# Row sums on one core: a tail of 10 rows in place of 16, whose last piece is shared by two adders

## The chip, the core and the metric

The kernel runs on one core of a Trainium2 chip. The metric is the device time of one execution in microseconds (us), as the median of several runs. The engines that appear here are VectorE (DVE), ScalarE (ACT), GpSimd (POOL) and SyncE (SP). SP issues every DMA of this kernel, so all of them stand in one queue, which 16 DMA engines work off.

## The reference

```python
def setup_inputs():
    batch, seq, dim = 32, 512, 1024
    return {"x": np.random.randn(batch, seq, dim).astype(np.float32), "divisor": float(dim)}

def reference(x, divisor):
    return (np.sum(x, axis=-1) / divisor).astype(np.float32)
```

The input has 16,384 rows of 1,024 numbers, 67.1 MB in all; each row is summed and scaled by 1/1024.

## The kernel before, in words

Each of the 128 partitions gets 128 rows of `D` = 1024 numbers. `F` = 15 of them come from the front of `x` (`x_first`, results in `res0`); the other `W` = 113 lie behind one another for each partition, and of these `M` = 97 form the main part (`x_main`, results in `res`) and the last `L` = 16 the tail (`x_last`, results in `fin`; `res` and `fin` are parts of one tile, `every`).

The list `loads` holds the large loads in order: the main part in loads of 2, five times 16, and 15 rows, then the 15 rows of `x_first`, then the first two loads of the tail. They rotate over three buffers `bulk0` to `bulk2` of 16 rows. The first two are issued at the very start. SP issues each later one when the adders are done with the buffer's previous load (the third waits for the first to land instead). Then SP issues two small loads of the tail, `pa` (into the tile `tail`) and `pb`, which have places of their own. Loads follow one another in the queue in this order.

Two adders share the rows. DVE sums all rows of a large load with one reduction (`reduce_sum`, line 217), but in the last main load and in `x_first` ACT takes the last 4 and 6 rows, one activation with an accumulated output for each (`row_on_act`, line 185). DVE's reductions write unscaled sums, which POOL scales (lines 159 and 163). In the tail DVE takes single rows with `both_halves` (line 207): one operation adds the first half of a row to its second half and accumulates over the columns, in two instructions, the main one and an accumulator read. ACT takes other rows of the tail.

The tail's pieces do not end at row ends; their limits are in `ends` and set by `c10`, `c14` and `c15`. Row 10 is split over the two tail loads: DVE sums its head into `part` and adds that when it sums the rest. Of row 14, ACT sums the head into a column just ahead of `pa`, and then sums that column and the rest as one piece. DVE sums row 15's head, at the end of `pa`, into a column just behind `pb`, and then sums `pb` with that column and a zero that POOL wrote at the start. A carry of this kind increments the semaphore of the piece that it is added to, so that the adder waits for 16 increments of the load and one of the carry: ACT's on `in_pa`, DVE's on `in_pb`.

Three stores take the results out: `o_first` (line 149) after POOL's scaling, `o_main` (line 152) with all columns of `every` up to `E` as soon as all but the last two rows are done, and `o_last` (line 240) with the remaining columns when both adders have counted up `done`.

Of the kernel before, what the change touches and what calls it, by code (L numbers as in the profile page):

```python
# [10 lines left out]
AX = mybir.AxisListType.X  # L11
# [24 lines left out]
def kernel(  # L36
# [6 lines left out]
    nc = tc.nc  # L43
    nc.at_finalize(start_loads_at_once)
    xf = x.flatten_outer_dims()
    N, D = xf.shape
    P = nc.NUM_PARTITIONS
    scale = 1.0 / float(divisor)
    J = N // P
    assert J * P == N  # L50

    F, L = 15, 16
    M = J - F - L
    W = M + L
    x_first = bass.AP(tensor=x.tensor, offset=0, ap=[[F * D, P], [1, F * D]])
    x_main = bass.AP(tensor=x.tensor, offset=P * F * D, ap=[[W * D, P], [1, M * D]])
    x_last = bass.AP(tensor=x.tensor, offset=P * F * D + M * D, ap=[[W * D, P], [1, L * D]])
    o_first = bass.AP(tensor=out.tensor, offset=0, ap=[[F, P], [1, F]])
    E = M + L - 2
    o_main = bass.AP(tensor=out.tensor, offset=P * F, ap=[[W, P], [1, E]])  # L60
    o_last = bass.AP(tensor=out.tensor, offset=P * F + E, ap=[[W, P], [1, 2]])

    def room(name, *shape):
        return nc.alloc_sbuf_tensor(name, [P, *shape], F32).ap()
# [5 lines left out]
    bulk = [room(f"bulk{i}", 16 * D) for i in range(3)]  # L70
# [1 line left out]

    c10, c14, c15 = 640, 288, 608
    ends = [0, 10 * D + c10, 14 * D + c14, 15 * D + c15, 16 * D]
    tail = room("tail", 7 * 256)
    pa, row14 = tail[:, 256 : 256 + ends[3] - ends[2]], tail[:, 255 : 256 + D - c14]
    pb = room("pb", 512)[:, : D - c15 + 2]
    part = room("part", 1)  # L80
    res0 = room("res0", F)
    every = room("every", W)
    res, fin = every[:, :M], every[:, M:]
# [4 lines left out]
    loads = []  # L88
    sems = {}

    def sem(name):
        sems[name] = nc.alloc_semaphore(name)
        return sems[name]

    in_bulk = [sem(f"in_bulk{i}") for i in range(3)]
    in_pa, in_pb = (sem(f"in_{n}") for n in ("pa", "pb"))
    out_first, out_main = sem("out_first"), sem("out_main")
    dve, act, pool = sem("by_dve"), sem("by_act"), sem("by_pool")
    done = sem("done")
    landed = nc.alloc_semaphore("landed")  # L100

    main = [(2, 0)] + [(16, 0)] * 5 + [(15, 4)]
    first = [(15, 6)]
    assert sum(r for r, _ in first) == F and sum(r for r, _ in main) == M
    for rows_of, src, dst in ((main, x_main, res), (first, x_first, res0)):
        j = 0
        for rows, on_act in rows_of:
            t = bulk[len(loads) % 3][:, : rows * D]
            loads.append((t, in_bulk[len(loads) % 3], src[:, j * D : (j + rows) * D], on_act, dst[:, j : j + rows]))
            j += rows  # L110
    for k in range(2):
        t = bulk[len(loads) % 3][:, : ends[k + 1] - ends[k]]
        loads.append((t, in_bulk[len(loads) % 3], x_last[:, ends[k] : ends[k + 1]], 0, None))


    for t, s, src, *_ in loads[:2]:
# [6 lines left out]
    done_dve, done_act = {}, {}  # L123
    a = 0
    for k, (t, s, src, on_act, dst) in enumerate(loads[:-2]):
        a += on_act
        done_dve[k], done_act[k] = k + 1, a
    arrived, seen = [], {}
    for t, s, *_ in loads:
        seen[s.num] = seen.get(s.num, 0) + 16  # L130
# [4 lines left out]
    for k, (t, s, src, *_) in enumerate(loads):  # L135
# [7 lines left out]
                nc.sync.wait_ge(act, done_act[k - 3])  # L143
            nc.sync.wait_ge(s, arrived[k] - 16)
        nc.sync.dma_start(out=t, in_=src).then_inc(s, 16)
    nc.sync.dma_start(out=pa, in_=x_last[:, ends[2] : ends[3]]).then_inc(in_pa, 16)
    nc.sync.dma_start(out=pb[:, : D - c15], in_=x_last[:, ends[3] : ends[4]]).then_inc(in_pb, 16)
    nc.sync.wait_ge(pool, 3)
    nc.sync.dma_start(out=o_first, in_=res0).then_inc(out_first, 16)
    nc.sync.wait_ge(act, done_act[len(loads) - 3] + 5)  # L150
    nc.sync.wait_ge(dve, done_dve[len(loads) - 3] + 10)
    nc.sync.dma_start(out=o_main, in_=every[:, :E]).then_inc(out_main, 16)


    nc.gpsimd.memset(pb[:, D - c15 :], 0.0).then_inc(pool)  # L155
    k = len(main) - 1
    nc.gpsimd.wait_ge(dve, done_dve[k])
    nc.gpsimd.wait_ge(act, done_act[k])
# [5 lines left out]


    (t8, s8, *_), (t9, s9, *_) = loads[-2:]
    head10, rest10 = t8[:, 10 * D :], t9[:, : D - c10]
    head14 = t9[:, 4 * D - c10 :]

    def row8(r):  # L170
        return t8[:, r * D : (r + 1) * D]

    def row9(r):
        return t9[:, (r - 10) * D - c10 : (r - 9) * D - c10]

    a = 0

    def row_on_act(src, by, dst, count=act):  # L180
        nonlocal a
        if a >= len(junk):
            nc.scalar.wait_ge(act, a - len(junk) + 1)
        scratch = junk[a % len(junk)][:, : src.shape[-1]]
        nc.scalar.activation(scratch, src, COPY, scale=by, accum_out=dst).then_inc(count)  # L185
        a += 1

    for k, (t, s, src, on_act, dst) in enumerate(loads[:-2]):
        rows = t.shape[1] // D
# [2 lines left out]
                nc.scalar.wait_ge(s, arrived[k])  # L192
            row_on_act(t[:, r * D : (r + 1) * D], 1.0, dst[:, r : r + 1])
    nc.scalar.wait_ge(s8, arrived[-2])
    for r in range(6, 10):
        row_on_act(row8(r), scale, fin[:, r : r + 1])
    nc.scalar.wait_ge(s9, arrived[-1])
    row_on_act(row9(13), scale, fin[:, 13:14])
    row_on_act(head14, 1.0, row14[:, :1], in_pa)
    nc.scalar.wait_ge(in_pa, 17)  # L200
    row_on_act(row14, scale, fin[:, 14:15], done)

    def both_halves(dst, src, by=scale, ahead=0.0):
        h = src.shape[-1] // 2
        return nc.vector.tensor_tensor_reduce(  # L207
            out=src[:, :h], in0=src[:, :h], in1=src[:, h:], scale=by, scalar=ahead,
            op0=ADD, op1=ADD, accum_out=dst,
        )  # L210

    d = 0
    for k, (t, s, src, on_act, dst) in enumerate(loads[:-2]):
        m = t.shape[1] // D - on_act
        nc.vector.wait_ge(s, arrived[k])
        rows = t[:, : m * D].rearrange("p (r d) -> p r d", d=D)
        nc.vector.reduce_sum(out=dst[:, :m], in_=rows, axis=AX).then_inc(dve)  # L217
        d += 1
    nc.vector.wait_ge(s8, arrived[-2])
    both_halves(part, head10).then_inc(dve)  # L220
    d += 1
    ahead10 = d
    for r in range(6):
        both_halves(fin[:, r : r + 1], row8(r)).then_inc(dve)
        d += 1
    nc.vector.wait_ge(s9, arrived[-1])
    nc.vector.wait_ge(dve, ahead10)
    both_halves(fin[:, 10:11], rest10, ahead=part).then_inc(dve)
    for r in (11, 12):
        both_halves(fin[:, r : r + 1], row9(r)).then_inc(dve)  # L230
    d += 3
    nc.vector.wait_ge(in_pa, 17)
    nc.vector.wait_ge(pool, 1)
    both_halves(pb[:, D - c15 : D - c15 + 1], pa[:, D - c14 :], 1.0).then_inc(in_pb)
    nc.vector.wait_ge(in_pb, 17)
    both_halves(fin[:, 15:], pb).then_inc(done)


    nc.sync.wait_ge(done, 2)
    nc.sync.dma_start(out=o_last, in_=every[:, E:]).then_inc(landed, 16)  # L240
    for s in (out_main, out_first):
# [40 lines left out]
```

## Time and profile before

| what | value |
|---|---|
| median of 3 runs | 160.26 us (160.24 to 160.31) |
| the profiled execution, its time | 160.4 us |
| its span, from the first to the last instruction | 159.1 us |
| DVE busy | 116.7 us (73%) |
| ACT busy | 18.6 us (12%) |
| POOL busy | 1.0 us (1%) |
| the loads' and stores' queue | 67.18 MB, 98.2% of 16 engines' span |
| read from HBM | 67.11 MB, 422 GB/s over the span |

The span begins with the first instruction of the program and ends with its last. In the views, a line such as L207 is a line of the kernel file; a helper's operations all have the helper's line, so rows are told apart by their tiles, their shapes and their order. `CUSTOM_DVE_ANT_0` is the main instruction of `both_halves` (its shape shows half the columns that it sums), `DVE_READ_ACCUMULATOR2_ANT` its accumulator read. `SPq` lines are DMA issues, and their duration is that of the issue alone. Buffer numbers are left out of names, so `bulk` is any of the three buffers.

### The profile page before, as it was taken

To read this page: it belongs to the slowest core of one execution; us is meant where nothing else is said; L and a number is where in the kernel's file an instruction comes from. 1 tells how busy PE (TensorE), PEld (TensorE's weight loads), DVE (VectorE), ACT (ScalarE), POOL (GpSimd) and SP (SyncE) were. 2 spreads that over 40 slices of the span, in tenths; PEclk is the share of its full clock that TensorE was granted. 3 is DMA by queue.
4 is the path that set the end of the run, shared out by engine and by line. 5 is a ranking of instruction groups with operands and counts; after the bars stand their busy time and mean duration, and the time that the engine had idled before them with its cause. 6 is when DMAs were issued, how large, how long until landed. Compare 5 with 4: busy or idle time off the path is not lost.

```text
span 159.1 us, 145 instructions
## 1 busy us (share of the span) xinstructions
DVE 116.7 (73%) x32; ACT 18.6 (12%) x35; POOL 1.0 (1%) x7
## 2 busy tenths in 40 slices
DVE  0500009999499994999949999499989990399296
ACT  3000000000000000000000000000009100392196
POOL 0000000000000000000000000000000001000000
DMA  7996996997979969969969969959995999889794
GB/s 249 542 527 264 527 527 264 527 461 330 527 346 445 527 264 527 527 264 527 527 264 527 527 264 527 494 247 494 494 494 247 494 494 494 350 350 525 311 421 169
DMA packets 2161, 67.18 MB, mean 422 GB/s; under 512 B 625, under 2 KB 753, under 8 KB 881
## 3 DMA queue, kind: packets, MB, share of 16 engines
q1 hardware_dynamic: 2160, 67.18, 98.2%
q14 instruction: 1, 0.00, 0.0%
HBM read 67.11 MB, written 0.07 MB: 422 GB/s over the span
## 4 chain that ended last, share of the span: by engine, by line
DMA 67%; DVE 31%; another core or an unknown queue 1%; issue 0%
DMA bulk<-in_x_dram 67%; DVE every L217 29%; DVE bulk L207 1%; DVE pb L207 0%; DVE tail L207 0%; DVE every L207 0%
## 5 line engine op out<-in xcount | busy, mean ns | idle before, releaser
L217 DVE TENSOR_REDUCE every<-bulk 128x16 f32<-128x16384 f32 (+2 forms) x7 | 100.3, 14325 | 31.2 <-DMA bulk<-in_x_dram 31.2
L185 ACT ACTIVATE junk<-bulk 128x1024 f32<-128x1024 f32 (+1 forms) x16 | 15.6, 972 | 136.9 <-DMA bulk<-in_x_dram 136.8
L217 DVE TENSOR_REDUCE res<-bulk 128x9 f32<-128x9216 f32 x1 | 9.8, 9754 | 6.3 <-DMA bulk<-in_x_dram 6.3
L207 DVE CUSTOM_DVE_ANT_0 bulk<-bulk 128x512 f32<-128x512 f32 (+1 forms) x9 | 5.5, 664 | 3.1 <-DMA bulk<-in_x_dram 3.1
L185 ACT ACTIVATION_READ_ACCUMULATOR junk<-bulk 128x1 f32 x16 | 3.0, 186 | 0.0
L185 ACT ACT_TABLE_LOAD x1 | 1.3, 1283 | 1.9 <-PEq L120 1.9
L159 POOL TENSOR_SCALAR every<-every 128x97 f32<-128x97 f32 x1 | 0.5, 465 | 129.5 <-DVE every L217 129.5
L207 DVE DVE_READ_ACCUMULATOR2_ANT every<- 128x1 f32 x10 | 0.8, 82 | 0.0
L185 ACT ACTIVATE junk<-tail 128x737 f32<-128x737 f32 x1 | 0.8, 789 | 0.0
L207 DVE CUSTOM_DVE_ANT_0 bulk<-bulk,part 128x192 f32<-128x192 f32 x1 | 0.4, 420 | 0.2 <-DMA bulk<-in_x_dram 0.2
L207 DVE CUSTOM_DVE_ANT_0 tail<-tail 128x304 f32<-128x304 f32 x1 | 0.5, 476 | 0.0
L207 DVE CUSTOM_DVE_ANT_0 pb<-pb 128x209 f32<-128x209 f32 x1 | 0.4, 379 | 0.1
L163 POOL TENSOR_SCALAR res<-res 128x15 f32<-128x15 f32 x1 | 0.3, 263 | 15.7 <-DVE res L217 15.7
L185 ACT ACTIVATION_READ_ACCUMULATOR junk<-tail 128x1 f32 x1 | 0.2, 185 | 0.0
L155 POOL MEMSET pb<- 128x2 f32 x1 | 0.1, 100 | 1.5 <-POOLq L120 1.5
L263 POOL MEMSET const-bfloat16-1.0<- 128x1 bf16 x1 | 0.1, 102 | 0.0
L263 POOL MEMSET const-uint8-127<- 128x1 uint8 x1 | 0.1, 101 | 0.0
L263 POOL MEMSET const-float32-0.0<- 128x1 f32 x1 | 0.1, 98 | 0.2 <-issue 0.2
L263 POOL MEMSET const-float32-1.0<- 128x1 f32 x1 | 0.1, 98 | 0.0
L207 DVE DVE_READ_ACCUMULATOR2_ANT pb<- 128x1 f32 x1 | 0.1, 83 | 0.0
L207 DVE DVE_READ_ACCUMULATOR2_ANT part<- 128x1 f32 x1 | 0.1, 81 | 0.0
## 6 DMA issues: line engine op xcount, KB each, us to landing
bulk<-in_x_dram SPq DMA_DIRECT2D x2, 7680.0 KB, 38.9
bulk<-in_x_dram SPq DMA_DIRECT2D x1, 5440.0 KB, 31.9
bulk<-in_x_dram SPq DMA_DIRECT2D x1, 1872.0 KB, 23.5
bulk<-in_x_dram SPq DMA_DIRECT2D x1, 1024.0 KB, 4.9
tail<-in_x_dram SPq DMA_DIRECT2D x1, 672.0 KB, 24.8
pb<-in_x_dram SPq DMA_DIRECT2D x1, 208.0 KB, 24.9
bulk<-in_x_dram SPq DMA_DIRECT2D x5, 40.7
out_dram<-every SPq DMA_DIRECT2D x1, 55.5 KB, 1.6
```

The lines of the kernel that those rows point to most:

```text
L155: nc.gpsimd.memset(pb[:, D - c15 :], 0.0).then_inc(pool)
L159: nc.gpsimd.tensor_scalar_mul(out=res, in0=res, scalar1=scale).then_inc(pool)
L163: nc.gpsimd.tensor_scalar_mul(out=res0, in0=res0, scalar1=scale).then_inc(pool)
L185: nc.scalar.activation(scratch, src, COPY, scale=by, accum_out=dst).then_inc(count)
L207: return nc.vector.tensor_tensor_reduce(out=src[:, :h], in0=src[:, :h], in1=src[:, h:], scale=by, scalar=ahead, op0=ADD, op1=ADD, accum_ou ...
L217: nc.vector.reduce_sum(out=dst[:, :m], in_=rows, axis=AX).then_inc(dve)
L263: nc = _bacc.Bacc("TRN2", target_bir_lowering=False, num_devices=1)
```

## The change

The tail has 10 rows instead of 16. Of the six rows that leave it, five go to the first load (7 rows instead of 2) and one to the last main load (16 instead of 15, of which DVE sums 12 and ACT 4). `M` becomes 103.

The tail's columns are no longer loaded in order. Its first load begins inside row 3 (from column 340 of that row) and goes to the end of row 9; its second holds rows 0 and 1 and 144 columns of row 2; then `p3` holds columns 144 to 983 of row 2; and the last piece, `p4`, holds the last 40 columns of row 2 and the first 340 of row 3, so it lies in the middle of the tail's data. ACT finishes row 2 from it and DVE row 3.

Four carried sums belong to that piece. DVE sums the rest of row 3 into a column behind the piece, and two parts of row 2 (`row2_y`, 144 columns, and `row2_u`, 640 columns) into columns ahead of it; ACT sums a third part of row 2 (`row2_v`, 200 columns). All four carries and the load increment one semaphore, `in_p4`, and both last additions wait for 16 + 4. DVE's last addition covers 342 columns (340, a carry and a zero), ACT's 43 (3 carries and 40).

In the load of `x_first`, DVE sums its 9 rows one at a time with `both_halves` instead of with one reduction. The last store takes the 8 columns of rows 2 to 9, and `o_main` the columns up to row 1; it waits for 3 rows of ACT and 5 of DVE behind the large loads.

```diff
-    F, L = 15, 16
+    F, L = 15, 10
...
-    E = M + L - 2
+    E = M + 2
...
-    c10, c14, c15 = 640, 288, 608
-    ends = [0, 10 * D + c10, 14 * D + c14, 15 * D + c15, 16 * D]
-    tail = room("tail", 7 * 256)
-    pa, row14 = tail[:, 256 : 256 + ends[3] - ends[2]], tail[:, 255 : 256 + D - c14]
-    pb = room("pb", 512)[:, : D - c15 + 2]
-    part = room("part", 1)
+    y2, u2, a2, c3 = 144, 640, 40, 340
+    ends = [3 * D + c3, L * D, 0, 2 * D + y2, 3 * D - a2]
+    p3 = room("p3", 1024)[:, : ends[4] - ends[3]]
+    n4 = a2 + c3
+    piece = room("piece", 768)
+    p4 = piece[:, 256 : 256 + n4]
+    row2_end, row3_head = piece[:, 253 : 256 + a2], piece[:, 256 + a2 : 256 + n4 + 2]
...
-    main = [(2, 0)] + [(16, 0)] * 5 + [(15, 4)]
+    main = [(7, 0)] + [(16, 0)] * 5 + [(16, 4)]
...
+        by_rows = k == len(loads) - 3
+        done_dve[k], done_act[k] = k + (t.shape[1] // D - on_act if by_rows else 1), a
...
-    nc.sync.dma_start(out=pa, in_=x_last[:, ends[2] : ends[3]]).then_inc(in_pa, 16)
-    nc.sync.dma_start(out=pb[:, : D - c15], in_=x_last[:, ends[3] : ends[4]]).then_inc(in_pb, 16)
+    nc.sync.dma_start(out=p3, in_=x_last[:, ends[3] : ends[4]]).then_inc(in_p3, 16)
+    nc.sync.dma_start(out=p4, in_=x_last[:, ends[4] : ends[0]]).then_inc(in_p4, 16)
...
-    nc.sync.wait_ge(act, done_act[len(loads) - 3] + 5)
-    nc.sync.wait_ge(dve, done_dve[len(loads) - 3] + 10)
+    nc.sync.wait_ge(act, done_act[len(loads) - 3] + 3)
+    nc.sync.wait_ge(dve, done_dve[len(loads) - 3] + 5)
...
-    nc.gpsimd.memset(pb[:, D - c15 :], 0.0).then_inc(pool)
+    nc.gpsimd.memset(row3_head[:, c3 + 1 :], 0.0).then_inc(pool)
...
+    every_carry = 16 + 4
...
     nc.scalar.wait_ge(s8, arrived[-2])
-    for r in range(6, 10):
+    for r in (8, 9):
         row_on_act(row8(r), scale, fin[:, r : r + 1])
     nc.scalar.wait_ge(s9, arrived[-1])
-    row_on_act(row9(13), scale, fin[:, 13:14])
-    row_on_act(head14, 1.0, row14[:, :1], in_pa)
-    nc.scalar.wait_ge(in_pa, 17)
-    row_on_act(row14, scale, fin[:, 14:15], done)
+    row_on_act(row1, scale, fin[:, 1:2])
+    nc.scalar.wait_ge(in_p3, 16)
+    row_on_act(row2_v, 1.0, row2_end[:, 2:3], in_p4)
+    nc.scalar.wait_ge(in_p4, every_carry)
+    row_on_act(row2_end, scale, fin[:, 2:3], done)
...
+            for r in range(m):
+                both_halves(dst[:, r : r + 1], t[:, r * D : (r + 1) * D], 1.0).then_inc(dve)
     nc.vector.wait_ge(s8, arrived[-2])
-    both_halves(part, head10).then_inc(dve)
...
-    for r in range(6):
+    both_halves(row3_head[:, c3 : c3 + 1], row3_rest, 1.0).then_inc(in_p4)
+    for r in (4, 5, 6, 7):
         both_halves(fin[:, r : r + 1], row8(r)).then_inc(dve)
...
     nc.vector.wait_ge(s9, arrived[-1])
-    nc.vector.wait_ge(dve, ahead10)
-    both_halves(fin[:, 10:11], rest10, ahead=part).then_inc(dve)
-    for r in (11, 12):
-        both_halves(fin[:, r : r + 1], row9(r)).then_inc(dve)
...
-    nc.vector.wait_ge(in_pa, 17)
+    both_halves(row2_end[:, :1], row2_y, 1.0).then_inc(in_p4)
+    both_halves(fin[:, :1], row0).then_inc(dve)
+    nc.vector.wait_ge(in_p3, 16)
     nc.vector.wait_ge(pool, 1)
-    both_halves(pb[:, D - c15 : D - c15 + 1], pa[:, D - c14 :], 1.0).then_inc(in_pb)
-    nc.vector.wait_ge(in_pb, 17)
-    both_halves(fin[:, 15:], pb).then_inc(done)
+    both_halves(row2_end[:, 1:2], row2_u, 1.0).then_inc(in_p4)
+    nc.vector.wait_ge(in_p4, every_carry)
+    both_halves(fin[:, 3:4], row3_head).then_inc(done)
```

More of the change, by code (lines that the diff above doesn't have):

```diff
@@ L58 @@
     o_first = bass.AP(tensor=out.tensor, offset=0, ap=[[F, P], [1, F]])
-    E = M + L - 2
+    E = M + 2
     o_main = bass.AP(tensor=out.tensor, offset=P * F, ap=[[W, P], [1, E]])
-    o_last = bass.AP(tensor=out.tensor, offset=P * F + E, ap=[[W, P], [1, 2]])
+    o_last = bass.AP(tensor=out.tensor, offset=P * F + E, ap=[[W, P], [1, W - E]])
     def room(name, *shape):
@@ L95 @@
     in_bulk = [sem(f"in_bulk{i}") for i in range(3)]
-    in_pa, in_pb = (sem(f"in_{n}") for n in ("pa", "pb"))
+    in_p3, in_p4 = (sem(f"in_{n}") for n in ("p3", "p4"))
     out_first, out_main = sem("out_first"), sem("out_main")
@@ L111 @@
     for k in range(2):
-        t = bulk[len(loads) % 3][:, : ends[k + 1] - ends[k]]
-        loads.append((t, in_bulk[len(loads) % 3], x_last[:, ends[k] : ends[k + 1]], 0, None))
+        t = bulk[len(loads) % 3][:, : ends[2 * k + 1] - ends[2 * k]]
+        loads.append((t, in_bulk[len(loads) % 3], x_last[:, ends[2 * k] : ends[2 * k + 1]], 0, None))
     for t, s, src, *_ in loads[:2]:
@@ L126 @@
         a += on_act
-        done_dve[k], done_act[k] = k + 1, a
+        by_rows = k == len(loads) - 3
+        done_dve[k], done_act[k] = k + (t.shape[1] // D - on_act if by_rows else 1), a
     arrived, seen = [], {}
@@ L166 @@
     (t8, s8, *_), (t9, s9, *_) = loads[-2:]
-    head10, rest10 = t8[:, 10 * D :], t9[:, : D - c10]
-    head14 = t9[:, 4 * D - c10 :]
+    row3_rest = t8[:, : D - c3]
     def row8(r):
-        return t8[:, r * D : (r + 1) * D]
-    def row9(r):
-        return t9[:, (r - 10) * D - c10 : (r - 9) * D - c10]
+        return t8[:, (r - 3) * D - c3 : (r - 2) * D - c3]
+    row0, row1, row2_y = t9[:, :D], t9[:, D : 2 * D], t9[:, 2 * D :]
+    row2_u, row2_v = p3[:, :u2], p3[:, u2:]
+    every_carry = 16 + 4
     a = 0
@@ L210, in both_halves @@
         )
-    d = 0
     for k, (t, s, src, on_act, dst) in enumerate(loads[:-2]):
@@ L215 @@
         nc.vector.wait_ge(s, arrived[k])
-        rows = t[:, : m * D].rearrange("p (r d) -> p r d", d=D)
-        nc.vector.reduce_sum(out=dst[:, :m], in_=rows, axis=AX).then_inc(dve)
-        d += 1
+        if k < len(loads) - 3:
+            rows = t[:, : m * D].rearrange("p (r d) -> p r d", d=D)
+            nc.vector.reduce_sum(out=dst[:, :m], in_=rows, axis=AX).then_inc(dve)
+        else:
+            for r in range(m):
+                both_halves(dst[:, r : r + 1], t[:, r * D : (r + 1) * D], 1.0).then_inc(dve)
     nc.vector.wait_ge(s8, arrived[-2])
-    both_halves(part, head10).then_inc(dve)
-    d += 1
-    ahead10 = d
-    for r in range(6):
+    both_halves(row3_head[:, c3 : c3 + 1], row3_rest, 1.0).then_inc(in_p4)
+    for r in (4, 5, 6, 7):
         both_halves(fin[:, r : r + 1], row8(r)).then_inc(dve)
-        d += 1
     nc.vector.wait_ge(s9, arrived[-1])
-    nc.vector.wait_ge(dve, ahead10)
-    both_halves(fin[:, 10:11], rest10, ahead=part).then_inc(dve)
-    for r in (11, 12):
-        both_halves(fin[:, r : r + 1], row9(r)).then_inc(dve)
-    d += 3
-    nc.vector.wait_ge(in_pa, 17)
+    both_halves(row2_end[:, :1], row2_y, 1.0).then_inc(in_p4)
+    both_halves(fin[:, :1], row0).then_inc(dve)
+    nc.vector.wait_ge(in_p3, 16)
     nc.vector.wait_ge(pool, 1)
-    both_halves(pb[:, D - c15 : D - c15 + 1], pa[:, D - c14 :], 1.0).then_inc(in_pb)
-    nc.vector.wait_ge(in_pb, 17)
-    both_halves(fin[:, 15:], pb).then_inc(done)
+    both_halves(row2_end[:, 1:2], row2_u, 1.0).then_inc(in_p4)
+    nc.vector.wait_ge(in_p4, every_carry)
+    both_halves(fin[:, 3:4], row3_head).then_inc(done)
     nc.sync.wait_ge(done, 2)
```

## The prediction, before the changed kernel ran

> **What bounds the kernel now.** I read the chain that ended last first.
>
> ```profile
> DMA 67%; DVE 31%; another core or an unknown queue 1%; issue 0%
> DMA bulk<-in_x_dram 67%; DVE every L217 29%; DVE bulk L207 1%; DVE pb L207 0%; DVE tail L207 0%; DVE every L207 0%
> ```
>
> The loads are two thirds of it; the DVE share is wide additions that free a buffer for a load which then stands in a queue that is still full. The timeline shows that: a 16-row addition starts as its load lands, and ends before the next one lands.
>
> ```profile
> 43.50 17.22 DVE L217 TENSOR_REDUCE every<-bulk 128x16 f32<-128x16384 f32 x1 [2.10 <-DMA bulk<-in_x_dram]
> 62.83 17.22 DVE L217 TENSOR_REDUCE every<-bulk 128x16 f32<-128x16384 f32 x1 [2.11 <-DMA bulk<-in_x_dram]
> ...
> 101.47 17.22 DVE L217 TENSOR_REDUCE every<-bulk 128x16 f32<-128x16384 f32 x1 [2.09 <-DMA bulk<-in_x_dram]
> ...
> 137.77 9.75 DVE L217 TENSOR_REDUCE res<-bulk 128x9 f32<-128x9216 f32 x1 [6.31 <-DMA bulk<-in_x_dram]
> ```
>
> From 43.50 to 101.47 us 48 rows arrive: 1.2077 us a row. The queue has no gap, so up to the tail the time is 128 rows at one rate, before and after. What is left is the stretch from the last landing on. It stands in the timeline of the tail (start, duration, engine, line):
>
> ```profile
> 150.62 0.49 DVE L207 CUSTOM_DVE_ANT_0 bulk<-bulk 128x320 f32<-128x320 f32 x1 [3.09 <-DMA bulk<-in_x_dram]
> ...
> 151.03 0.69 DVE L207 CUSTOM_DVE_ANT_0 bulk<-bulk 128x512 f32<-128x512 f32 x1
> ...
> 154.10 0.68 DVE L207 CUSTOM_DVE_ANT_0 bulk<-bulk 128x512 f32<-128x512 f32 x1
> ...
> 155.03 1.03 ACT L185 ACTIVATE junk<-bulk 128x1024 f32<-128x1024 f32 x1
> 155.03 0.42 DVE L207 CUSTOM_DVE_ANT_0 bulk<-bulk,part 128x192 f32<-128x192 f32 x1 [0.24 <-DMA bulk<-in_x_dram]
> ...
> 155.37 0.69 DVE L207 CUSTOM_DVE_ANT_0 bulk<-bulk 128x512 f32<-128x512 f32 x1
> ...
> 156.08 0.39 ACT L185 ACTIVATE junk<-bulk 128x288 f32<-128x288 f32 x1
> 156.42 0.19 ACT L185 ACTIVATION_READ_ACCUMULATOR junk<-bulk 128x1 f32 x1
> ...
> 156.64 0.79 ACT L185 ACTIVATE junk<-tail 128x737 f32<-128x737 f32 x1
> 156.64 0.48 DVE L207 CUSTOM_DVE_ANT_0 tail<-tail 128x304 f32<-128x304 f32 x1
> 156.76 0.34 SPq L152 DMA_DIRECT2D out_dram<-every  x1
> 157.04 0.08 DVE L207 DVE_READ_ACCUMULATOR2_ANT pb<- 128x1 f32 x1
> 157.23 0.38 DVE L207 CUSTOM_DVE_ANT_0 pb<-pb 128x209 f32<-128x209 f32 x1
> 157.37 0.18 ACT L185 ACTIVATION_READ_ACCUMULATOR junk<-tail 128x1 f32 x1
> ...
> 157.65 0.33 SPq L240 DMA_DIRECT2D out_dram<-every  x1
> ```
>
> Here `pa` lands at 156.64 and starts ACT's row 14 and DVE's 304-column carry together. `pb` lands at 157.23 and starts DVE's last addition, 0.38 us. SP issues the last store at 157.65, and the span ends at 159.1, 1.4 us on. The windows agree: the loads have left the DMA engines just after 156.6 and then only landing and stores remain (busy time of DVE, ACT, POOL; clock; DMA share; GB/s).
>
> ```profile
> 155.00:156.60 1.60, 1.57 (x6) 1.57 (x4) 0.00 (x0) 1.00 0.99 397
> 156.60:157.30 0.70, 0.59 (x5) 0.66 (x2) 0.00 (x0) 1.00 0.20 38
> ```
>
> **Arrivals after the change.** When the load of `x_first` lands, 118 rows are in instead of 112: 137.77 + 6 x 1.2077 = 145.02. The next load had 10.625 rows in 150.62 - 137.77 = 12.85 us, so 6.668 rows take 8.06: 153.08. The next had 3.656 rows in 4.41, the bulk rate; 2.141 rows take 2.59: 155.67. `pa` (1.3125 rows) took 1.61, 0.025 above the rate, `pb` (0.406) took 0.59, 0.10 above. For `p3` (0.820 rows) I take 0.04 above, between them and nearer to `pa`, by its size: 0.99 + 0.04, 156.70. For `p4` (0.371 rows) I take `pb`'s 0.10: 0.45 + 0.10, 157.25. The last landing is thus 0.02 later than 157.23, within 0.08 either way by those two excesses.
>
> **The tail on DVE.** In a row of additions the starts are 0.614 us apart for 512-column halves (151.03 to 154.10, five steps), and 0.41 after a 320-column one, so 1.06 ns a column. Row 3's 342 columns take 0.43, rows 4 to 7 2.46, `row2_y` (72 columns) 0.15, row 0 0.61. From 153.08 DVE reaches `row2_u` at 156.73, 0.03 after `p3` is there. That carry has 320 columns: as at 150.62, 0.41 to the accumulator read and 0.08 for it, so 157.22. An engine that waits for its own count resumes 0.03 later (ACT: 156.42 + 0.19 = 156.61, next start 156.64): 157.25, the moment of `p4`. The last addition has 171 columns instead of 209: 0.38 - 0.04 = 0.34, and DVE is done at 157.59 instead of 157.61.
>
> Not in the trace are a 72-column addition and a wait on DVE that is already satisfied. The first lies between its columns alone, 0.08, and the 0.34 from 155.03 to 155.37 of the 192-column form; I take the line through the two like forms. The second costs between nothing and the 0.08 by which neighbouring additions overlap, twice (for the second bulk load and for `p3`). I take nothing, since ACT waits for its own old counts between rows and keeps 1.04 us starts either way. The late end of these is 0.19 + 0.16, the early end 0.07.
>
> [...]
>
> **The tail on ACT.** Row 1 starts at 155.67, `row2_v` 1.05 later, at 156.72. From 288 columns (156.08 to 156.61) to 200, at (0.79 - 0.39) / 449 = 0.88 ns a column, it takes 0.45: 157.17, ahead of DVE. The last step has 43 columns: 0.91 (156.64 to 157.55) less 694 x 0.88 ns leaves 0.30, done at 157.55. So DVE still ends last; the sharing takes 38 columns from it.
>
> **What lies under cover.** Putting nine rows singly in place of the 9.75 us reduction takes 9 x 0.614 = 5.5 us and ends at 150.6; DVE then waits until 153.08, so this gains nothing. If it weren't there, the reduction would end at 154.77 and cost 1.7. The first load makes DVE begin at 10.92 instead of 4.88, and SP's third load goes out then, with 16 rows (19.3 us) still queued. The last wide addition, 12 rows, ends about 139.8; then the second tail load, `p3` and `p4` are issued, 13 us before the queue needs them; a missed issue would cost its lateness one for one. POOL's scaling and the first store come near 151.8 instead of 147.97; the store stands behind `p4` in the same queue, as behind `pb` now (issued 147.97, landed 9.4 us later). The wide store waits for row 0 and row 1, both near 156.83, and is issued about 156.85 against 156.76; SP is free 0.34 later, before the last store, so it costs nothing. The last store's eight columns instead of two go out in as many pieces; its 1.4 us are kept, since the 444-byte pieces took only 1.6.
>
> **The sum.** The last addition's end moves by -0.02. The profiled execution took 160.40 (span 159.1 and 1.3 around it), so it gives 160.38; the median of the runs lies 0.14 lower, so 160.24. With the bounds, -0.09 to +0.33: 160.17 to 160.59. About 0.2%, or 0.32 us, is what a measurement here can tell from no change.
>
> **Rivals.**
> (1) Slower: DVE, not the load, becomes last. Both final additions now wait for one count of 16 + 4, so the slowest carry holds up both. In the seven links from 153.08 to `row2_u`'s accumulator read neighbours must keep overlapping by 0.08; if the mixture of lengths and waits breaks that overlap at every link, it costs 7 x 0.08 = 0.56, no slack is left to absorb it, and the time is 160.24 + 0.56 = 160.80. It decides from a delay of 0.34 us on. For it: the carry and the landing tie at 157.25. Against it: all steps of 150.62 to 154.10 overlap, as do two of the three after 155.03. 0.09. [...]
> (2) Slower: the tail's loads begin at places that are no multiple of 16 columns (3412 and 3032; all starts now are multiples of 32). If that made packets as slow as `pb`'s, 0.59 / 0.406 = 1.45 us a row, the 6.668 rows would take 1.62 more: 161.86. Against it: the 444-byte stores start at any multiple of 4 bytes, and the trace's packet records give 22 to 28 ns for one, on the line through the aligned 1,664 and 60 bytes (69 and 11 ns). 0.04. [...]
> (3) Faster: a longer first load rides out the start better. The packet records show that each engine's first 8 KB packet took 0.64 to 1.26 us, later ones 0.31. If most of the least such loss, 0.33, were a cost of short first packets, the time would be near 159.91. Against it: it looks like a first access, which any size pays once, and behind it packets follow without gaps. 0.07.
> (4) The change doesn't do what it says: the last piece is shared, but DVE keeps 342 of its columns. That is in my sum.
>
> **How the numbers follow.** The forecast has 0.80. It lies within 0.2%, so same is 0.80, slower 0.09 + 0.04, faster 0.07. The range takes the forecast's own 160.17 to 160.59, and reaches down to 160.05 towards rival (3).
>
> **What would show it.** Right: DVE's 7-row reduction near 10.9, `x_first`'s rows from 145.0, the tail from 153.1, `row2_u` starting within 0.1 of `p3`'s landing, the last addition near 157.25 for 0.34, the last store issued near 157.63. Wrong in (1): the last addition starts over 0.1 after `p4`'s landing. Wrong in (2): over 8.3 us between 145.0 and the first tail addition. Wrong in (3): the first reduction ends its wait before 10.7. Anything else that moves the last landing by over 0.3 makes the prediction wrong.

## The result, and the profile after

The changed kernel took 160.63 us in the median (14 runs, 160.54 to 160.82), the kernel before 160.33 beside it (14 runs, 160.20 to 160.88). The medians differ by 0.30. The ratio, estimated from all these runs, is 1.0017 with a 95% interval of 1.0009 to 1.0025: slower by 0.27 us, within 0.14 to 0.40. That is less than the 0.2% I had set as the smallest difference to be told, yet clear of its interval, and the median lies 0.04 above the end of my range. The profiled execution took 160.6 with a span of 159.3.

The chain that ended last, from the page after:

```profile
DMA 74%; DVE 24%; issue 0%
DMA bulk<-in_x_dram 74%; DVE every L220 22%; DVE bulk L210 2%; DVE p L210 0%; DVE piece L210 0%; DVE every L210 0%
```

It is still the loads, then DVE. The timeline of the stream (start, duration, engine, line; each of DVE's entries starts as its load lands):

```profile
10.94 7.62 DVE L220 TENSOR_REDUCE every<-bulk 128x7 f32<-128x7168 f32 x1 [10.94 <-DMA bulk<-in_x_dram]
30.23 17.22 DVE L220 TENSOR_REDUCE every<-bulk 128x16 f32<-128x16384 f32 x1 [11.67 <-DMA bulk<-in_x_dram]
...
107.59 17.22 DVE L220 TENSOR_REDUCE every<-bulk 128x16 f32<-128x16384 f32 x1 [2.08 <-DMA bulk<-in_x_dram]
...
145.11 0.69 DVE L210 CUSTOM_DVE_ANT_0 bulk<-bulk 128x512 f32<-128x512 f32 x1 [5.24 <-DMA bulk<-in_x_dram]
```

The first load lands where forecast (10.94 against 10.92). The 64 rows from 30.23 to 107.59 take 1.2088 us each instead of 1.2077, and `x_first`'s rows start at 145.11 instead of 145.02. The tail:

```profile
150.63 0.08 DVE L210 DVE_READ_ACCUMULATOR2_ANT res<- 128x1 f32 x1
...
153.19 0.52 DVE L210 CUSTOM_DVE_ANT_0 bulk<-bulk 128x342 f32<-128x342 f32 x1 [2.48 <-DMA bulk<-in_x_dram]
...
153.63 0.69 DVE L210 CUSTOM_DVE_ANT_0 bulk<-bulk 128x512 f32<-128x512 f32 x1
...
155.81 1.03 ACT L187 ACTIVATE junk<-bulk 128x1024 f32<-128x1024 f32 x1 [0.43 <-DMA bulk<-in_x_dram]
156.08 0.08 DVE L210 DVE_READ_ACCUMULATOR2_ANT every<- 128x1 f32 x1
156.08 0.23 DVE L210 CUSTOM_DVE_ANT_0 bulk<-bulk 128x72 f32<-128x72 f32 x1
...
156.24 0.69 DVE L210 CUSTOM_DVE_ANT_0 bulk<-bulk 128x512 f32<-128x512 f32 x1
...
156.85 0.08 DVE L210 DVE_READ_ACCUMULATOR2_ANT every<- 128x1 f32 x1
156.92 0.34 ACT L187 ACTIVATE junk<-p 128x200 f32<-128x200 f32 x1
156.92 0.49 DVE L210 CUSTOM_DVE_ANT_0 p<-p 128x320 f32<-128x320 f32 x1
157.01 0.34 SPq L154 DMA_DIRECT2D out_dram<-every  x1
157.20 0.18 ACT L187 ACTIVATION_READ_ACCUMULATOR junk<-p 128x1 f32 x1
157.34 0.08 DVE L210 DVE_READ_ACCUMULATOR2_ANT piece<- 128x1 f32 x1
157.46 0.21 ACT L187 ACTIVATE junk<-piece 128x43 f32<-128x43 f32 x1
157.46 0.34 DVE L210 CUSTOM_DVE_ANT_0 piece<-piece 128x171 f32<-128x171 f32 x1
157.60 0.19 ACT L187 ACTIVATION_READ_ACCUMULATOR junk<-piece 128x1 f32 x1
157.72 0.08 DVE L210 DVE_READ_ACCUMULATOR2_ANT every<- 128x1 f32 x1
157.83 0.33 SPq L239 DMA_DIRECT2D out_dram<-every  x1
```

The nine rows end at 150.63 + 0.08, 2.5 us before the first tail load lands, as forecast. Then each arrival is later: 153.19 (forecast 153.08), 155.81 (155.67), `p3` 156.92 (156.70). DVE could go on at 156.85, with the accumulator read of row 0, and waits for `p3`, whose last increment by a DMA engine comes at 156.90. `row2_u` takes 0.54 from its start to the next (forecast 0.52), so the last addition starts at 157.46 instead of 157.25. In the semaphore records `p4`'s last increment by a DMA engine comes at 157.38, that of ACT's carry at 157.39 and that of DVE's at 157.43, so here DVE's carry ends last, by 0.04. The last addition takes 0.34, as forecast, ACT's 43 columns end before it, and the store is issued at 157.83 against 157.65 before.

The windows of the same stretch (busy time of DVE, ACT, POOL; clock; DMA share; GB/s):

```profile
155.70:156.70 1.00, 1.00 (x5) 0.89 (x1) 0.00 (x0) 1.00 0.99 361
156.70:157.50 0.80, 0.77 (x5) 0.73 (x5) 0.00 (x0) 1.00 0.10 24
```

At 156.7 the DMA share falls from 0.99 to 0.10 (before, at 156.6, from 0.99 to 0.20), and DVE is busy for nearly all of both windows.

### The profile page after: what moved, and what is told of

Read it like the earlier page. It is cut to its first block, busy times and chain, and to the rows that moved or that the text cites. A ratio compares the mean times of both kernels' runs of the same rounds, so it can differ in the third digit from the quotient of the medians.

```text
span 159.3 us, 152 instructions
## 1 busy us (share of the span) xinstructions
DVE 116.8 (73%) x43; ACT 16.0 (10%) x31; POOL 1.0 (1%) x7
## 4 chain that ended last, share of the span: by engine, by line
DMA 74%; DVE 24%; issue 0%
DMA bulk<-in_x_dram 74%; DVE every L220 22%; DVE bulk L210 2%; DVE p L210 0%; DVE piece L210 0%; DVE every L210 0%
## 5 line engine op out<-in xcount | busy, mean ns | idle before, releaser
L220 DVE TENSOR_REDUCE every<-bulk 128x16 f32<-128x16384 f32 (+2 forms) x7 | 106.7, 15239 | 33.2 <-DMA bulk<-in_x_dram 33.2
L187 ACT ACTIVATE junk<-bulk 128x1024 f32<-128x1024 f32 x13 | 13.2, 1013 | 139.8 <-DMA bulk<-in_x_dram 139.8
L210 DVE CUSTOM_DVE_ANT_0 bulk<-bulk 128x512 f32<-128x512 f32 (+2 forms) x16 | 9.3, 650 | 7.7 <-DMA bulk<-in_x_dram 7.7
L187 ACT ACTIVATION_READ_ACCUMULATOR junk<-bulk 128x1 f32 x13 | 2.4, 187 | 0.0
L161 POOL TENSOR_SCALAR every<-every 128x103 f32<-128x103 f32 x1 | 0.5, 478 | 137.9 <-DVE every L220 137.9
L210 DVE DVE_READ_ACCUMULATOR2_ANT res<- 128x1 f32 x9 | 0.8, 84 | 0.0
L210 DVE CUSTOM_DVE_ANT_0 p<-p 128x320 f32<-128x320 f32 x1 | 0.5, 493 | 0.0
```

Of the source, the lines that this page charges most:

```text
L161: nc.gpsimd.tensor_scalar_mul(out=res, in0=res, scalar1=scale).then_inc(pool)
L210: return nc.vector.tensor_tensor_reduce(out=src[:, :h], in0=src[:, :h], in1=src[:, h:], scale=by, scalar=ahead, op0=ADD, op1=ADD, accum_ou ...
```

## The experiments

Two theories of the 0.27 us:

- **A, the start:** the longer first load costs time in the stream.
- **B, the tail:** the new tail's pieces, starts and carries cost it.

All runs, as medians against the kernel before on the same chip. The ratio is not the quotient of these medians but an estimate of its own, and mostly a smaller one:

| run | first load | tail | us | against before | ratio (95% interval) |
|---|---|---|---|---|---|
| changed kernel, first comparison | 7 rows | new | 160.63 | +0.30 | 1.0017 (1.0009 to 1.0025) |
| e1_first7 | 7 | old | 160.55 | +0.09 | 1.0003 (0.9994 to 1.0011) |
| e2_first2 | 2 | new | 160.49 | +0.03 | 1.0001 (0.9992 to 1.0010) |
| e3_aligned | 7 | new, other cuts | 160.65 | +0.19 | 1.0007 (0.9999 to 1.0016) |
| e4_rows | 2 | old | 160.49 | +0.03 | 1.0002 (0.9993 to 1.0011) |
| e5_after (changed kernel again) | 7 | new | 160.64 | +0.16 | 1.0007 (0.9998 to 1.0016) |
| e6_first16 | 16 | old | 161.24 | +0.76 | 1.0041 (1.0027 to 1.0055) |
| e7_odd | 7 | new | 160.73 | +0.25 | 1.0011 (1.0001 to 1.0020) |
| e8_first2_aligned | 2 | new, other cuts | 160.63 | +0.15 | 1.0004 (0.9994 to 1.0013) |
| e9_first14 | 14 | old | 160.56 | +0.20 | 1.0009 (1.0001 to 1.0018) |
| e10_first1 | 1 | old | 160.39 | +0.03 | 1.0001 (0.9993 to 1.0010) |
| e11_old_odd | 2 | old, other cuts | 160.46 | +0.10 | 1.0000 (0.9991 to 1.0008) |
| e12_short_carry | 7 | new | 160.64 | +0.28 | 1.0017 (1.0008 to 1.0026) |

### The first load alone, 7 rows (e1_first7)

```diff
-    main = [(2, 0)] + [(16, 0)] * 5 + [(15, 4)]
+    main = [(7, 0)] + [(16, 0)] * 4 + [(11, 0), (15, 4)]
```

> The old tail, with the change's first load alone: 7 rows first, and 11 rows in place of 16 in a later main load. Theory A (the start: longer first packets leave the 16 DMA engines further apart, and the last one of them carries its lag to the end): slower than before by 0.15 to 0.3 us. Theory B (the tail: its pieces, landings and carries cost the time): within 0.08 us of before.

Its +0.09 decides nothing: it lies between the two expectations. The profile leans towards A:

```profile
137.91 9.76 DVE L217 TENSOR_REDUCE res<-bulk 128x9 f32<-128x9216 f32 x1 [6.32 <-DMA bulk<-in_x_dram]
...
157.35 0.38 DVE L207 CUSTOM_DVE_ANT_0 pb<-pb 128x209 f32<-128x209 f32 x1
```

`x_first`'s rows start 0.14 later than before (137.77), and the last addition 0.12 later (157.23), after 19.44 us of tail against 19.46. One profile decides little here: in the two of the changed kernel, `x_first`'s rows start 0.05 apart (145.11, and 145.06 in e5_after below).

### The new tail with the old start (e2_first2)

```diff
-    main = [(7, 0)] + [(16, 0)] * 5 + [(16, 4)]
+    main = [(2, 0)] + [(16, 0)] * 5 + [(5, 0), (16, 4)]
```

> The changed tail of 10 rows and the single rows, but a first load of 2 rows as before, with the other 5 rows in a load of their own late in the main part. Theory A: within 0.1 us of before (the additional load's eight packets per engine may cost 0.06). Theory B: slower than before by 0.2 to 0.35 us, like the changed kernel.

+0.03 with an additional load is what A says, and not the 0.2 of B. The upper end of the interval is 0.16 us, so a smaller cost of the tail stays possible.

### The new tail with even starts (e3_aligned)

```diff
-    y2, u2, a2, c3 = 144, 640, 40, 340
+    y2, u2, a2, c3 = 128, 640, 64, 320
```

> The changed kernel with its cuts moved by at most 24 columns, so that every load of the tail starts at a multiple of 64 columns (256 bytes). Theory A and theory B without a price on odd starts: as the changed kernel, 0.2 to 0.35 us slower than before. Theory B with a price on odd starts: 0.1 us or more faster than the changed kernel, and the first tail load takes 0.03 us or more less beside its rows.

+0.19 lies just under the first expectation, and the interval, from nothing to 0.26 us, fits either, so the runs put no price on the starts. In its timeline `p3`'s addition starts 11.74 us after `x_first`'s rows, against 11.81 in the changed kernel:

```profile
145.16 0.69 DVE L210 CUSTOM_DVE_ANT_0 bulk<-bulk 128x512 f32<-128x512 f32 x1 [5.18 <-DMA bulk<-in_x_dram]
...
156.90 0.49 DVE L210 CUSTOM_DVE_ANT_0 p<-p 128x320 f32<-128x320 f32 x1
...
157.44 0.33 DVE L210 CUSTOM_DVE_ANT_0 piece<-piece 128x161 f32<-128x161 f32 x1
```

### The single rows alone (e4_rows)

```diff
...
-        rows = t[:, : m * D].rearrange("p (r d) -> p r d", d=D)
-        nc.vector.reduce_sum(out=dst[:, :m], in_=rows, axis=AX).then_inc(dve)
+        if k < len(loads) - 3:
+            ...
+        else:
+            for r in range(m):
+                both_halves(dst[:, r : r + 1], t[:, r * D : (r + 1) * D], 1.0).then_inc(dve)
```

> The kernel before with only the 9 rows of x_first summed one at a time. Both theories: within 0.08 us of before, DVE's nine rows taking 5.6 us instead of 9.75 and DVE waiting 4 us longer for the first tail load. If this alone is slower by 0.15 or more, the row operations disturb the loads and both theories fall.

As expected, nothing: +0.03, and the last addition starts at 157.26.

```profile
137.72 0.69 DVE L208 CUSTOM_DVE_ANT_0 bulk<-bulk 128x512 f32<-128x512 f32 x1 [6.26 <-DMA bulk<-in_x_dram]
...
157.26 0.38 DVE L208 CUSTOM_DVE_ANT_0 pb<-pb 128x209 f32<-128x209 f32 x1
```

### The changed kernel again, as an anchor (e5_after)

> The changed kernel itself, beside the next three and the kernel before on one chip. All theories: slower than before by 0.15 to 0.35 us; in its profile the last addition starts 0.56 us after the start of row2_u, which starts as p3 lands.

+0.16 at the low end of what was expected, with an interval that just reaches 1. Its last addition starts 0.55 after `row2_u`:

```profile
145.06 0.69 DVE L210 CUSTOM_DVE_ANT_0 bulk<-bulk 128x512 f32<-128x512 f32 x1 [5.23 <-DMA bulk<-in_x_dram]
...
156.87 0.49 DVE L210 CUSTOM_DVE_ANT_0 p<-p 128x320 f32<-128x320 f32 x1
...
157.42 0.34 DVE L210 CUSTOM_DVE_ANT_0 piece<-piece 128x171 f32<-128x171 f32 x1
```

`x_first`'s rows start 0.04 later than forecast here, against 0.09 in the first profile. And in this execution the last increment that the last addition waits for is `p4`'s landing (157.39), not DVE's carry (157.38). The two comparisons of the same kernel, +0.30 and +0.16, show how little a single one can carry.

### A first load of 16 rows (e6_first16)

```diff
-    main = [(2, 0)] + [(16, 0)] * 5 + [(15, 4)]
+    main = [(16, 0)] * 5 + [(2, 0), (15, 4)]
```

> The kernel before with a first load of 16 rows and the 2-row load put late, so the start's packets are eight times as long as before. Theory A (a longer first load costs time): slower than before by 0.3 us or more, clearly more than the 0.09 seen with 7 rows. Theory B (the tail): within 0.1 us of before.

+0.76 looks like A, but most of it is a side effect of the edit. The short load in sixth place makes SP issue the load of `x_first` late. SP's own entries between 110 and 121 us, merged (the first of the two is `x_first`'s), and then DVE's additions of the last main load and of `x_first`:

```profile
116.49 2.52 SPq L145 DMA_DIRECT2D bulk<-in_x_dram  x2
```

```profile
119.79 11.89 DVE L217 TENSOR_REDUCE every<-bulk 128x11 f32<-128x11264 f32 x1 [1.14 <-DMA bulk<-in_x_dram]
...
138.49 9.75 DVE L217 TENSOR_REDUCE res<-bulk 128x9 f32<-128x9216 f32 x1 [6.81 <-DMA bulk<-in_x_dram]
```

The same load's issue and the addition of the load ahead of it in the kernel before:

```profile
99.40 0.33 SPq L145 DMA_DIRECT2D bulk<-in_x_dram  x1
```

```profile
119.57 11.89 DVE L217 TENSOR_REDUCE every<-bulk 128x11 f32<-128x11264 f32 x1 [0.88 <-DMA bulk<-in_x_dram]
```

`x_first`'s load is issued 3.3 us before the one ahead of it lands, against 20.2 before. It then lands 18.70 us after that one instead of 18.20. I put these 0.50 down to the late issue; no run varied that alone. The load ahead of it lands 0.22 later than before, and that is what is left to the first load.

### Odd starts for the large loads (e7_odd)

```diff
-    x_first = bass.AP(tensor=x.tensor, offset=0, ...
-    x_main = bass.AP(tensor=x.tensor, offset=P * F * D, ...
+    x_first = bass.AP(tensor=x.tensor, offset=20, ...
+    x_main = bass.AP(tensor=x.tensor, offset=P * F * D + 20, ...
```

> The changed kernel with the main loads and the load of x_first starting 20 columns later in x, so that all large loads start off a 256-byte boundary, as the first tail load does; the sums of those rows are then those of other windows, and only the time is meant. If odd starts cost a share of the data's time, the stream to x_first's landing (145.1) grows by 1 us or more; if they cost a fixed piece per load, by 0.1 to 0.2 us over the eight loads; if nothing, the time is the changed kernel's within 0.08.

+0.25, in the range of the changed kernel, and `x_first`'s rows start at 145.17 against 145.11 and 145.06 in the two profiles of that kernel. No share of the data's time, and no more than about 0.1 for eight loads.

### Both presumed costs taken out (e8_first2_aligned)

The edits of e2_first2 and e3_aligned together.

> The tail of 10 rows with every tail load starting at a multiple of 64 columns, and a first load of 2 rows as before, its other 5 rows in a load of their own late in the main part. If the first load and odd starts are the two costs: as before, plus about 0.06 for the additional load. If the carry chain of the tail (p3's landing to the last addition) is the cost: 0.1 to 0.2 slower than before all the same.

Inconclusive: the median is +0.15, the ratio 1.0004, and both expectations fit the interval. The profile:

```profile
145.20 0.69 DVE L210 CUSTOM_DVE_ANT_0 bulk<-bulk 128x512 f32<-128x512 f32 x1 [5.18 <-DMA bulk<-in_x_dram]
...
156.92 0.49 DVE L210 CUSTOM_DVE_ANT_0 p<-p 128x320 f32<-128x320 f32 x1
...
157.46 0.33 DVE L210 CUSTOM_DVE_ANT_0 piece<-piece 128x161 f32<-128x161 f32 x1
```

The last addition starts 12.26 us after `x_first`'s rows, as in e3_aligned (12.28), against 12.35 and 12.36 in the two profiles of the changed kernel.

### A long first load without the side effect (e9_first14)

```diff
-    main = [(2, 0)] + [(16, 0)] * 5 + [(15, 4)]
+    main = [(14, 0)] * 6 + [(13, 4)]
```

> The kernel before with main loads of 14 rows each (the last 13), so that the first load is long and every later one is still issued long before the queue needs it, which was not so in the 16-row trial. Theory A (a longer first load costs time, about 0.05 us a row): slower than before by 0.3 us or more. Theory B (the first load's length costs nothing by itself; the 16-row trial lost its time at the late load of x_first): within 0.12 us of before.

+0.20, and the interval excludes no difference. That is A by its sign and above B's 0.12, but less than A's 0.05 a row.

```profile
19.53 15.09 DVE L217 TENSOR_REDUCE every<-bulk 128x14 f32<-128x14336 f32 x1 [19.53 <-DMA bulk<-in_x_dram]
...
137.94 9.75 DVE L217 TENSOR_REDUCE res<-bulk 128x9 f32<-128x9216 f32 x1 [8.36 <-DMA bulk<-in_x_dram]
...
157.39 0.38 DVE L207 CUSTOM_DVE_ANT_0 pb<-pb 128x209 f32<-128x209 f32 x1
```

The first landing in the kernel before:

```profile
4.88 2.29 DVE L217 TENSOR_REDUCE every<-bulk 128x2 f32<-128x2048 f32 x1 [4.88 <-DMA bulk<-in_x_dram]
```

Here the first load lands at 19.53; 4.88 and 12 rows at 1.2077 give 19.37. `x_first`'s rows start 0.17 later than before, the last addition 0.16 later, and the tail between them takes 19.45 against 19.46.

### A first load of 1 row (e10_first1)

```diff
-    main = [(2, 0)] + [(16, 0)] * 5 + [(15, 4)]
+    main = [(1, 0)] + [(16, 0)] * 5 + [(16, 4)]
```

> The kernel before with a first load of 1 row and a last main load of 16, of which ACT takes 4. Theory A: 0.05 us faster than before, at the edge of what the interval shows. Theory B: within 0.08 us of before.

No gain in the runs: +0.03, as B says, though the interval reaches down to -0.11 us and holds A's 0.05 as well. Its profile has the earliest tail of all:

```profile
137.71 9.75 DVE L217 TENSOR_REDUCE res<-bulk 128x9 f32<-128x9216 f32 x1 [5.25 <-DMA bulk<-in_x_dram]
...
157.16 0.38 DVE L207 CUSTOM_DVE_ANT_0 pb<-pb 128x209 f32<-128x209 f32 x1
```

### Odd starts in the old tail (e11_old_odd)

```diff
-    c10, c14, c15 = 640, 288, 608
+    c10, c14, c15 = 660, 298, 618
```

> The kernel before with its three cuts of the tail moved by 10 to 20 columns, so that three of its tail loads start off a 256-byte and a 64-byte boundary. If odd starts of tail loads cost time: in the profile the mean landing of pb over the 16 DMA engines lies 19.51 to 19.54 us after that of x_first's load, instead of 19.44 to 19.47, and the time grows by 0.07. If the 0.07 is of the new tail's other sizes: 19.44 to 19.47 and no change of time.

The ratio is 1.0000, and `pb`'s addition starts 19.46 after `x_first`'s, exactly as before. In the landing records the means are 19.48 apart, between the two expectations: before, e1, e9 and e10 have 19.44 to 19.45, but e4_rows, whose starts are even, has 19.47. So an odd start costs at most 0.03 over these three loads, and nothing that shows in the runs.

```profile
137.82 9.76 DVE L217 TENSOR_REDUCE res<-bulk 128x9 f32<-128x9216 f32 x1 [6.30 <-DMA bulk<-in_x_dram]
...
157.28 0.37 DVE L207 CUSTOM_DVE_ANT_0 pb<-pb 128x204 f32<-128x204 f32 x1
```

### A shorter carry (e12_short_carry)

```diff
-    row2_u, row2_v = p3[:, :u2], p3[:, u2:]
+    row2_u, row2_v = p3[:, :240], p3[:, u2:]
```

> The changed kernel with row2_u cut from 640 to 240 columns, so that 400 columns of row 2 are left out of its sum and DVE's last carry is 0.2 us shorter. If that carry is what the last addition waits for: it starts within 0.04 us of p4's landing, instead of 0.05 to 0.09, and the time is 0.03 to 0.07 shorter than the changed kernel's 0.16 over before. If the landing bounds it: no change.

The kernel leaves 400 columns of row 2 out of its sum. In the profile the bound of DVE's carry is gone: its accumulator read ends at 157.15. The last addition now waits for two increments that come together, at 157.33: `p4`'s last one and that of ACT's carry, which the profile names.

```profile
156.87 0.28 DVE L210 CUSTOM_DVE_ANT_0 p<-p 128x120 f32<-128x120 f32 x1
...
157.07 0.08 DVE L210 DVE_READ_ACCUMULATOR2_ANT piece<- 128x1 f32 x1
157.14 0.19 ACT L187 ACTIVATION_READ_ACCUMULATOR junk<-p 128x1 f32 x1
...
157.36 0.34 DVE L210 CUSTOM_DVE_ANT_0 piece<-piece 128x171 f32<-128x171 f32 x1 [0.20 <-ACT junk L187]
```

It starts 0.49 after `row2_u`'s start instead of 0.54, so DVE's carry is worth up to 0.05; in e5_after it was worth nothing. The runs don't show a gain: +0.28 is no less than the changed kernel's own.

## Why the prediction was wrong

**What held.** The cover: the nine rows (done at 150.71, ahead of the landing at 153.19; +0.03 in e4_rows), the late first reduction (done at 18.56, the next load lands at 30.23), the later stores (the wide one issued at 157.01, the last at 157.83) and POOL (done at 151.80) held up nothing in the profile. On DVE the single terms were met: 342 columns 0.44 (0.43), `row2_y` 0.16 (0.15), the last addition 0.34, ACT's last step done before it. A wait that was already satisfied cost nothing there: `row2_y` starts at 156.08, together with the accumulator read of the row before it, although a wait for the second tail load (there since 155.81) stands between. Rival (1) as priced, with its 0.08 at every link, did not occur: six of the seven links still overlap, and the seventh is the wait for `p3`. In kind a little of it came: DVE's carry ended last, by 0.04 in one profile of the kernel and not in the other. Rival (2), priced at 1.62, is refuted by e7_odd and e11_old_odd for starts as such. They cost about 0.1 us at most for eight loads, and 0.00 by the starts, or 0.03 by the mean landings, for three. The 72-column addition itself lasts 0.23 in the trace, but the next one starts 0.16 behind its start, so the sum had to go by the starts.

**What failed first: "the queue has no gap, so up to the tail the time is 128 rows at one rate, before and after".** I took the first load's length to be free, but for rival (3), which had the sign wrong. Five kernels with a first load of 1 or 2 rows lie 0.03 to 0.15 above the one before in the runs (e2, e4, e8, e10, e11), and the seven comparisons with 7 or 14 rows lie 0.09 to 0.30 above it (e6 is left out for its late load). Five of those seven have the new tail, so the two tails have to be kept apart. The means of the medians' differences, with those of the ratios in brackets:

| tail | first load of 1 or 2 rows | first load of 7 or 14 rows |
|---|---|---|
| old | 0.05 (0.02): e4, e10, e11 | 0.15 (0.10): e1, e9 |
| new | 0.09 (0.04): e2, e8 | 0.24 (0.19): the other five |

So the runs give some 0.1 to 0.15 to the first load, and 0.04 to 0.09 to the tail. No single comparison tells such a difference, as its interval is 0.13 us or more either way.

The profiles put the first load's share ahead of the tail. With the old tail, `x_first`'s rows start at 137.71 to 137.82 with 1 or 2 rows first (before, e4, e10, e11), and at 137.91 and 137.94 with 7 and 14 (e1, e9). In the changed kernel they start 0.09 later than at the old rate (145.11), in e5_after and e12_short_carry, which are the same up to there, 0.04 later (145.06). Where in the stream this arises isn't settled. With 14 rows 0.16 is there at the first landing, with 7 rows (10.94) 0.02, but by the landing records the 2-row load's own landing lies anywhere from 4.55 to 5.00.

The landing records of the 16 DMA engines show more. DVE starts 0.02 after the last engine has landed (4.88 after 4.86 at the first landing before, 145.11 after 145.09 at `x_first` in the changed kernel), so a start has two parts: when the engines land in the mean, and how far the last one trails that mean. The mean of `x_first`'s load is 137.41 with 1 row first, 137.49 to 137.60 with 2 rows (five kernels), 137.54 to 137.72 with 7 (six kernels) and 137.61 with 14, with six rows at 1.2077 taken off for the new tail. Between 2 and 7 rows that is 0.05 on average. The last engine trails by 0.15 to 0.44, in no order by the first load's length, and mostly it is there from the first landing on: 0.29 there and 0.30 at `x_first` in the changed kernel, 0.20 at both in e5_after, 0.42 and 0.44 in e8. The changed kernel's profile is 0.09 late by this trailing alone, since its mean (137.54) is no later than the one before (137.57). Two kernels with a new tail and 2 rows first (e2, e8) have a late `x_first` as well, at 145.24 and 145.20, and that is trailing too: their means are 137.57 and 137.49, so their additional load costs nothing that shows there. So the runs bear out theory A's sign, and the means lean that way, but its mechanism, that longer packets leave the engines further apart, isn't borne out. How a longer first load costs time stays open.

**What failed second: the arrivals within the tail, and with them the tie at 157.25.** I gave `p3` an excess of 0.04 over its rows and `p4` one of 0.10. Measured by the starts, `p3` had 1.11 us, 0.12 over; by the landing records `p4` came 0.48 behind it, 0.03 over. The sum is about the one I had (0.15 against 0.14), but the split matters. `row2_u` can't start before `p3` and takes 0.54 from there, so the last addition comes 0.08 behind `p4`'s landing, where I had both at the same time. With the first two tail loads, 0.02 and 0.03 late, this makes the last addition start 12.35 after `x_first`'s rows, where I had 12.23. The last addition, shorter by 0.04, was in my sum. The tie itself nearly held, with everything later: DVE's carry, ACT's carry (which I had 0.08 ahead) and `p4`'s landing come within 0.05 of each other, and in e5_after the landing is the last of them. e12_short_carry shows that without DVE's carry 0.05 is gained and then ACT's carry and the landing bound.

Another 0.07 went in e3_aligned and e8_first2_aligned, which moved the cuts. The landing records show it well: `p4`'s mean landing lies 12.28 to 12.29 behind `x_first`'s in the five kernels with the changed kernel's cuts (after, e2, e5, e7, e12) and 12.21 to 12.22 in these two, near my 12.23. Whether the starts or the sizes of the pieces do that stays open, as e11_old_odd gives odd starts 0.03 at most, and the runs don't show the gain (e3 +0.19, e8 +0.15).

Some readings in the working were loose, without weight in the sum. The 0.03 from an engine's own count to its next start came from ACT at 156.64, where `pa` had also just landed (156.62 in the landing records); DVE's last carry now shows it, with 0.04 from the end of its accumulator read at 157.42 to 157.46. And in the packet records before, fifteen of the first sixteen packets took 0.64 to 1.26 and the other one 0.31, and of the packets that rival (3) puts at 0.31, the second sixteen of the first load still took up to 0.58. In the changed kernel the first sixteen packets, of 28 KB, took 1.21 to 1.94 where most later ones of that load took 1.06.

**The sum by what was measured:** -0.02 as forecast, 0.09 ahead of the tail and 0.12 in it give +0.19, the difference of the two profiled executions (159.3 to 159.1, the last stores at 157.83 and 157.65). In e5_after's profile the same terms are -0.02, 0.04 and 0.13, and its last store is issued at 157.79, 0.14 later than before. The runs' +0.27 and, in the second comparison, +0.11 by the ratios lie on either side. My range ended at the wrong place because its late bounds were all DVE's; the stream had none.

## What to carry to other kernels

When a kernel is one gapless stream, the stream itself needs a bound in the estimate, too: here the runs give some 0.1 to 0.15 of its 157 us to the first load, and the last addition became shorter by 0.04. In a tail that alternates landings and carries, look for the piece whose carry is as long as the next landing takes: I estimate that shortening the last piece then gains little, as the carry from the piece before it ends next (here the two carries and the landing came within 0.05 us; no run here shortened the piece). When a landing comes late, look at all 16 engines' increments before giving the lateness to an edit: how far the last one trails the mean differed by up to 0.3 us between the profiled executions here, as much as the whole effect. And in an experiment on the order of loads, keep each of them issued as early as before: in e6_first16 one that was issued 3.3 us ahead of the landing before it, instead of 20.2, landed 18.70 us behind that one instead of 18.20, and these 0.50 are more than the 0.22 that was left to the order.

## What the runs showed that I had not expected

A load that was issued 3.3 us before the one ahead of it landed took 18.70 us for what took 18.20 in the kernel before, although the queue was never empty by the issue times (e6_first16). In the packet records the first packet of that load was longer on 14 of the 16 DMA engines, up to 2.96 us instead of 2.27, as the first packets of the whole program were (1.21 to 1.94 instead of 1.06 in the changed kernel). That every load needs such a lead, and how long, wasn't tried.
